# A pool of transposed activations begins 480 bytes further on, and a bias table grows by 32 bytes

## The chip, the cores and the metric

The kernel runs on one core of one Trainium2 chip. The metric is the device time of one execution in microseconds, lower is better. The kernel before takes 1579.77 us (median of three runs, 1577.89 to 1583.2).

## The reference, cut to what matters

One layer of a decoder trunk on 1024 tokens of width 1024, in float32: layer norm, an input projection, two kinds of self-attention side by side, an output projection, cross-attention over 256 memory tokens, and a squared-ReLU MLP of width 4096, each followed by a residual and a layer norm.

```python
x = layer_norm(x, ln_emb_g, ln_emb_b)
h = x @ w_in[l] + b_in[l]
...
mix = jnp.concatenate([out_a, out_b], axis=-1) @ w_o[l] + b_o[l]
x = layer_norm(DN_ALPHA * x + mix, ln1_g[l], ln1_b[l])
ca = memory_cross_attention(x, mem, ...)
x = layer_norm(DN_ALPHA * x + ca, ln2_g[l], ln2_b[l])
f = jnp.square(jax.nn.relu(x @ w_up[l] + b_up[l])) @ w_down[l] + b_down[l]
x = layer_norm(DN_ALPHA * x + f, ln3_g[l], ln3_b[l])
```

## The kernel before

**Arithmetic.** Large products are made of three matmuls each (`mm3`, line 102): a float32 operand is split by ScalarE into a rounded high part, and by GpSimd or VectorE into the rest, the low part; high by high, high by low and low by high are summed in PSUM. In `PE.matmul(out, a, b)` the second operand, `a`, is the stationary one that is loaded as weights (PEld in the profile), and `b` the moving one. In a row of the profile the moving operand stands first: `b<-a,wh` is a moving tile `a` on stationary weights `wh`, `b<-wh,a` a moving tile `wh` on a stationary tile `a`; `b` before the arrow is a PSUM bank. Nearly all matmuls have 512 moving columns; the scores of the cross-attention have 256.

**Stages**, in order of time: input projection and indexer (to about 440 us of the span), the two self-attentions with the memory's projections beside them, the output projection `w_o` and layer norm 1 (about 581 to 700 us), cross-attention for two halves of the tokens (to about 900), `w_up` (about 905 to 1235) and `w_down` (to the end). `w_up` takes 16 steps of seven products of 12 matmuls (`up_product`, line 1096); `w_down` takes three chunks of seven products and a plain rest (`PLAIN`).

**Where tiles lie.** Each partition of on-chip memory is one range of bytes. Pools opened on the left stack upwards, pools on the right downwards. What matters here:

- `pw` (line 131, right): the weights' high parts `wh`, four buffers from byte 188,384, the low parts `wl` from 204,768, and raw weights `wr`. All of them lie 480 bytes beyond a multiple of 512.
- `pm` (line 345, right): `fb0` at 172,000 and `fb1` at 180,192, also 480 beyond a multiple of 512.
- `pact` (line 912, left): the activations, transposed, as `a0` to `a11`, 8,192 bytes each, from byte 71,680, which is 140 times 512. `BIG` (line 916) says that `a0` to `a11` come from `pact` and `fb0`, `fb1` from `pm`; all of them have the same shapes and uses.

- `xT` (line 188, left), the transposed input of the input projection, from byte 50,912, 224 beyond a multiple of 512: 256 bytes from the weights' place.

A slice for one matmul begins at a multiple of 512 bytes within its tile, so a tile's place within 512 bytes is that of all its operands. In `w_o` (`proj_tok`, line 929) and the cross-attention's output, activations are stationary and weights move; in the cross-attention's queries (line 1011) and in `w_up` the weights are stationary and activations move. In `w_up` five of the seven products move two `a` tiles (high and low), and the two with `T3` and `T4` move `fb0` or `fb1` as the high part and an `a` tile as the low part. In the chunks of `w_down` the `a` tiles hold raw quarters that VectorE adds and ScalarE, GpSimd and VectorE split into `wh` and `wl`; only its plain rest gives `a` tiles to TensorE.

**Order.** A planner orders every engine's instructions by a simulated timeline; each engine then runs its own in that order. The pools `pr` and `pact` take over the memory of the self-attention's tiles, each tile waiting for the old tiles that lay under it.

Of the kernel before, what the change touches and what calls it, by code (L numbers as in the profile page):

```python
# [10 lines left out]
F32 = mybir.dt.float32  # L11
# [10 lines left out]
P = 128  # L22
# [12 lines left out]
def kernel(ctx: ExitStack, tc: tile.TileContext, x, mem, ln_emb_g, ln_emb_b, w_in, b_in,  # L35
# [4 lines left out]
    PE, ACT, DVE, POOL, SP = nc.tensor, nc.scalar, nc.vector, nc.gpsimd, nc.sync  # L40
# [4 lines left out]
    def pool(name, bufs=1, **kw):  # L45
        return ctx.enter_context(tc.tile_pool(name=name, bufs=bufs, **kw))

    def sub_pool(name, side=None):
        st = ExitStack()
        kw = {} if side is None else {"side": side}  # L50
        return st, st.enter_context(tc.tile_pool(name=name, bufs=1, reuse_waits="tile", **kw))
# [137 lines left out]
    st0, p0 = sub_pool("p0")  # L189
# [86 lines left out]

    TW = 328
    TC = ((0, 640, 128), (128, 1280, 128), (256, 1920, 72))
    btok = p0.tile([P, TW], F32)
    for d0, s0, n in TC:  # L280
        SP.dma_start(btok[:, d0:d0 + n], row_src(b_in, s0, n))
    th = p0.tile([P, KT, TW], F32R)
# [627 lines left out]
    pst, psum = psum_pool("psd")  # L910
    pr = pool("pr", reuse_waits="tile")
    pact = pool("pact", reuse_waits="tile")
    xr = [pr.tile([P, D], F32, name=f"xr{i}") for i in range(NB)]
    ROW = ("row0", "row1", "row2")
    MM, TR = tuple("b%d" % i for i in range(6)), ("b6", "b7")
# [481 lines left out]
def _build(nc, arrays, inputs, **kw):  # L1397
    import numpy as _np
    args = []
    named = [(n, inputs[n]) for n in _INS] + [("bucket_rows", _bucket_rows())]  # L1400
    for name, v in named:
        a = _np.ascontiguousarray(v)
        arrays[f"in_{name}_dram"] = a
        args.append(nc.dram_tensor(f"in_{name}_dram", a.shape, mybir.dt.from_np(a.dtype), kind="ExternalInput").ap())
    for i, (shape, dtype) in enumerate(_OUTS):
        args.append(nc.dram_tensor(f"out_{i}_dram", shape, mybir.dt.from_np(_np.dtype(dtype)), kind="ExternalOutput").ap())
    with tile.TileContext(nc, schedule_with_timeline_sim=True) as tc:
        kernel(tc, *args, **kw)
# [11 lines left out]
```

## Time and profile before

| | |
|---|---|
| median of three runs | 1579.77 us |
| the profiled execution | 1573.87 us, its span 1572.0 us |
| TensorE matmuls busy | 1449.3 us, 92% of the span |
| VectorE, GpSimd, ScalarE busy | 74%, 54%, 51% |
| granted TensorE clock, mean | 0.967 of full speed |

PE is TensorE's matmuls, PEld its weight loads, DVE VectorE, ACT ScalarE, POOL GpSimd. L86 is the line of `mm` through which nearly all matmuls go, so matmuls are told apart by their tiles. A matmul's recorded duration overlaps those of its neighbours, since they are pipelined; the distance from one start to the next is what a matmul costs in a run of matmuls.

### The profile page before, as it was taken

How to read it: one execution, taken by the hardware profiler on the slowest of the kernel's cores; microseconds unless marked ns; L12 is line 12 of the kernel's file. 1: busy time of each engine (PE TensorE's matmuls, PEld its weight loads, DVE VectorE, ACT ScalarE, POOL GpSimd, SP SyncE). 2: the span in 40 equal slices, each digit the busy share in tenths (PEclk: the TensorE clock that was granted, in tenths of full speed). 3: DMA queues.
4: the chain of work that ended last, by engine and by line, in shares of the span. 5: the costliest groups of instructions: out<-in, count | busy, mean ns of one | idle time of the engine just before them, and what ended most of it. 6: DMA issues, size and time to landing. Idle time of an engine off the chain costs nothing. (4 is left out here: it accounts for less than half of the span.)

```text
span 1572.0 us, 22293 instructions
## 1 busy us (share of the span) xinstructions
PE 1449.3 (92%) x7190; PEld 1208.9 (77%) x7190; DVE 1165.3 (74%) x2442; ACT 798.3 (51%) x1665; POOL 847.4 (54%) x753
## 2 busy tenths in 40 slices
PE   5989998785998999899999979999999999999887
PEld 4877776765897987688888758888888887888666
DVE  8639899969687868985263495575544799988857
ACT  6336677664787864235334154545455444444422
POOL 6213856546556555666565585645445345454745
PEclk9999998986999999999999989999999999999999
DMA  6252445873748248633322133423333934420002
GB/s 218 75 161 68 135 134 154 247 237 93 211 137 241 94 154 267 185 103 105 101 82 84 42 102 121 138 103 129 113 106 100 395 110 134 145 70 1 27 32 103
DMA packets 139907, 206.63 MB, mean 131 GB/s; under 512 B 18055, under 2 KB 83086, under 8 KB 139790
## 3 DMA queue, kind: packets, MB, share of 16 engines
q1 hardware_dynamic: 139790, 205.21, 41.4%
q8 instruction: 57, 0.93, 0.3%
q14 instruction: 60, 0.49, 0.1%
HBM read 151.66 MB, written 52.45 MB: 130 GB/s over the span
## 5 line engine op out<-in xcount | busy, mean ns | idle before, releaser
L86 PE MATMUL b<-a,wh 128*128 128x512 f32 x1072 | 300.2, 402 | 8.8 <-DVE a L1075 8.1
L161 POOL TENSOR_TENSOR wl<-wr,wh 128x512 fp32r<-128x512 f32 x158 | 228.5, 1466 | 145.8 <-ACT wh L160 137.4
L86 PE MATMUL b<-wl,wh 128*128 128x512 f32 x1192 | 278.1, 393 | 13.5 <-POOL wl L1089 13.3
L86 PEld LDWEIGHTS b<-wl,wh 128*128 128x128 f32 x1192 | 224.9, 189 | 63.9 <-POOL wl L1089 16.3
L86 PEld LDWEIGHTS b<-a,wh 128*128 128x128 f32 x1072 | 203.5, 191 | 58.2 <-issue 8.9
L1089 POOL TENSOR_TENSOR wl<-a,wl 128x512 fp32r<-128x512 f32 x44 | 92.4, 2099 | 109.0 <-ACT wl L1088 99.2
L160 ACT ACTIVATE wh<-wr 128x512 fp32r<-128x512 f32 x136 | 81.1, 627 | 128.5 <-PE b L86 46.4
L1089 POOL TENSOR_TENSOR wh<-row,wh 128x512 fp32r<-128x512 f32 x72 | 98.1, 1368 | 88.5 <-ACT wh L1088 85.2
L86 PE MATMUL fill<-xT,wh 128*128 128x512 f32 (+1 forms) x416 | 126.8, 384 | 6.8 <-ACT wt L393 6.8
L86 PE MATMUL b<-wh,a 128*128 128x512 f32 (+1 forms) x416 | 122.5, 369 | 7.6 <-DVE a L761 5.6
L86 PE MATMUL b<-a,wl 128*128 128x512 f32 x400 | 123.0, 396 | 0.0
L1088 ACT ACTIVATE wh<-a 128x512 fp32r<-128x512 f32 x80 | 50.5, 631 | 111.5 <-PE b L86 82.0
L86 PEld LDWEIGHTS fill<-xT,wh 128*128 128x128 f32 x416 | 78.5, 195 | 23.0 <-ACT wt L393 8.3
L86 PEld LDWEIGHTS b<-wh,a 128*128 128x128 f32 x416 | 76.4, 191 | 22.8 <-DVE a L761 5.9
L1282 DVE TENSOR_TENSOR xr<-xr,b 128x512 f32<-128x512 f32 x132 | 81.5, 675 | 14.1 <-PE b L86 14.1
L86 PEld LDWEIGHTS b<-a,wl 128*128 128x128 f32 x400 | 75.0, 188 | 17.4
L86 PE MATMUL fill<-xT,wl 128*128 128x512 f32 (+1 forms) x208 | 79.8, 385 | 0.0
L1100 ACT ACTIVATE lt<-lt,colst 128x512 f32<-128x512 f32 x60 | 43.2, 722 | 68.1 <-DVE lt L1207 67.3
L86 PE MATMUL b<-wl,a 128*128 128x512 f32 (+1 forms) x208 | 76.2, 369 | 1.3 <-POOL wl L161 1.3
L1207 DVE TENSOR_TENSOR lt<-b,lt 128x512 f32<-128x512 f32 x80 | 53.3, 686 | 32.1 <-PE b L86 27.5
L769 DVE TENSOR_TENSOR PT<-tr,PT 128x512 fp32r<-128x512 f32 (+3 forms) x128 | 70.6, 576 | 8.7 <-ACT PT L768 8.4
L768 ACT ACTIVATE PT<-tr 128x512 fp32r<-128x512 f32 (+3 forms) x128 | 61.4, 507 | 25.1 <-PE tr L870 11.6
(327 smaller groups left out, 3664.8 us busy)
## 6 DMA issues: line engine op xcount, KB each, us to landing
row<-in_w_up_dram SPq DMA_DIRECT2D x32, 512.0 KB, 4.3
ff_d<-lt SPq DMA_DIRECT2D x28, 512.0 KB, 3.0
a<-in_w_down_dram SPq DMA_DIRECT2D x50, 256.0 KB, 5.2
a<-ff_d SPq DMA_DIRECT2D x46, 256.0 KB, 3.5
wr<-in_xa_wkv_dram SPq DMA_DIRECT2D x32, 256.0 KB, 4.0
wr<-in_w_o_dram SPq DMA_DIRECT2D x32, 256.0 KB, 3.2
wr<-in_xa_wq_dram SPq DMA_DIRECT2D x32, 256.0 KB, 2.7
wr<-vwo_d SPq DMA_DIRECT2D x32, 256.0 KB, 2.8
```

Source lines behind the costliest of these rows:

```text
L86: i = PE.matmul(o, a, b, start=start, stop=stop)
L160: ACT.activation(hs, raw, AF.Copy)
L161: lo[i % len(lo)].tensor_tensor(out=ls, in0=raw, in1=f(hs), op=OP.subtract)
L768: ACT.activation(PT[0], pt, AF.Copy)
L769: DVE.tensor_tensor(out=PT[1], in0=pt, in1=f(PT[0]), op=OP.subtract)
L1088: ACT.activation(hl[:, 0], raw, AF.Copy)
L1089: return lo.tensor_tensor(out=hl[:, 1], in0=raw, in1=f(hl[:, 0]), op=OP.subtract)
L1100: ACT.activation(c, src, AF.Relu, bias=colst[:, C_UP + col:C_UP + col + 1])
L1207: DVE.tensor_tensor(out=o, in0=a, in1=b, op=op)
L1282: DVE.tensor_tensor(out=xs, in0=xs, in1=p, op=op)
```

## The change

The table of token biases `btok` gets eight more float32 columns, which nothing uses, so every tile of the first stage's pool `p0` that comes after it lies 32 bytes further on. The pool `pact` gets a first tile of 120 float32 (480 bytes) that GpSimd fills with zeros and nothing reads, so `a0` to `a11` begin at byte 72,160, 480 beyond a multiple of 512. `pact` then ends at 170,464, still below `fb0`. The new first tile lies over one old tile, the second query tile `qs` that the last attention unit reads; `a0` lay over it before and still does. No other tile lies over another set of old tiles than before.

```diff
-    btok = p0.tile([P, TW], F32)
+    btok = p0.tile([P, TW + 8], F32, name="btok")[:, :TW]
...
     pact = pool("pact", reuse_waits="tile")
+
+    POOL.memset(pact.tile([P, 120], F32, name="shift"), 0.0)
     xr = [pr.tile([P, D], F32, name=f"xr{i}") for i in range(NB)]
```

## Rows read from the trace of the kernel before

**Rows 1.** The page: span, and each engine's busy time.

```profile
span 1572.0 us, 22293 instructions
PE 1449.3 (92%) x7190; PEld 1208.9 (77%) x7190; DVE 1165.3 (74%) x2442; ACT 798.3 (51%) x1665; POOL 847.4 (54%) x753
```

**Rows 2.** Busy us by stretch (x matmuls started), granted clock as PEclk.

```profile
600.00:700.00 100.00, 91.10 (x399) 72.45 (x399) 92.78 (x108) 37.27 (x58) 65.72 (x38) 0.97 0.55 166
700.00:900.00 200.00, 200.00 (x1020) 167.67 (x1018) 96.90 (x157) 76.43 (x172) 115.18 (x109) 1.00 0.27 88
950.00:1200.00 250.00, 250.00 (x1077) 201.62 (x1076) 143.00 (x186) 126.85 (x208) 125.25 (x92) 1.00 0.35 116
1300.00:1450.00 150.00, 149.78 (x660) 123.91 (x661) 136.43 (x195) 64.12 (x112) 66.86 (x43) 1.00 0.26 87
1450.00:1500.00 50.00, 38.66 (x158) 30.85 (x157) 41.03 (x67) 19.09 (x35) 39.92 (x13) 0.91 0.07 21
```

**Rows 3.** Waits of PE: who for whom, us in total, times, longest.

```profile
PE b L86 <- POOL wl L1089: 13.3, 5, 6.6
```

**Rows 4.** Timeline of PE in `w_o`: start us, us, instruction, count.

```profile
592.27 0.39 PE L86 MATMUL b<-wh 128*128 128x512 f32 x1
...
597.72 0.39 PE L86 MATMUL b<-wh,a 128*128 128x512 f32 x1
...
603.31 0.39 PE L86 MATMUL b<-wh,fb 128*128 128x512 f32 x1
```

**Rows 5.** Timeline of PE in the input projection.

```profile
76.36 0.63 PE L86 MATMUL fill<-xT,wh 128*128 128x512 f32 x2
...
81.82 0.40 PE L86 MATMUL fill<-xT,wh 128*128 128x256 f32 x2
```

**Rows 6.** Timeline of PE in `w_up`.

```profile
1099.82 5.76 PE L86 MATMUL b<-a,wh 128*128 128x512 f32 x24
1105.42 0.40 PE L86 MATMUL b<-fb,wl 128*128 128x512 f32 x1
...
1108.20 5.75 PE L86 MATMUL b<-a,wh 128*128 128x512 f32 x24
```

**Rows 7.** Timeline of PE in `w_down`, one run of matmuls.

```profile
1329.83 110.55 PE L86 MATMUL b<-wl,wh 128*128 128x512 f32 x487
```

**Rows 8.** Timeline of PE in the plain rest of `w_down`.

```profile
1524.16 2.92 PE L86 MATMUL b<-a,a 128*128 128x512 f32 x12
1526.92 0.40 PE L86 MATMUL po<-fb,a 128*128 128x512 f32 x1
...
1529.71 2.92 PE L86 MATMUL b<-a,a 128*128 128x512 f32 x12
```

**Rows 9.** Instructions by form, whole span: xcount | busy us, mean ns | idle before.

```profile
L86 PE MATMUL b<-a,wh 128*128 128x512 f32 x1072 | 300.2, 402 | 8.8 <-DVE a L1075 8.1 <-DVE wr L1071 0.4 <-DVE rstd L116 0.3
L86 PE MATMUL b<-a,wl 128*128 128x512 f32 x400 | 123.0, 396 | 0.0
L86 PE MATMUL b<-wh,a 128*128 128x512 f32 x288 | 95.9, 406 | 7.6 <-DVE a L761 5.6 <-ACT a L760 2.0
L86 PE MATMUL b<-wl,a 128*128 128x512 f32 x144 | 58.2, 406 | 1.3 <-POOL wl L161 1.3
L86 PE MATMUL b<-wh,a 128*128 128x256 f32 x128 | 26.5, 286 | 0.0
L86 PE MATMUL lg<-bb,ident_r 128*128 128x256 f32 x96 | 19.9, 290 | 0.0
```

**Rows 10.** Timeline of POOL: after attention, and late in `w_down`; idle before in brackets.

```profile
587.79 3.37 POOL L161 TENSOR_TENSOR wl<-wr,wh 128x512 fp32r<-128x512 f32 x2 [12.01 <-ACT wh L160]
...
1486.42 11.51 POOL L1089 TENSOR_TENSOR wl<-a,wl 128x512 fp32r<-128x512 f32 x1 [1.60 <-ACT wl L1088]
```

**Rows 11.** DMA issues: xcount, KB each, median us to landing.

```profile
a<-in_w_down_dram SPq DMA_DIRECT2D x50, 256.0 KB, 5.2
fb<-in_w_down_dram SPq DMA_DIRECT2D x6, 256.0 KB, 5.2
```

## The prediction

> **What bounds the kernel now.** I read the page first: matmuls fill 1449.3 us of a span of 1572.0 us, VectorE 74%, GpSimd 54% [rows 1]. TensorE is the first suspect, but an average over stages is no proof, so I took busy time by stretch next [rows 2]. From 700 to 900 us and from 950 to 1200 us TensorE is busy without a break, at full granted clock, with VectorE at about half and GpSimd at 50 to 58%: there, and only there, a shorter matmul is a shorter kernel. From 600 to 700 us it is busy for 91.1 of 100 us. From 1300 to 1450 us it is full as well (149.78 of 150) but VectorE is at 136.43 of 150, so two engines are near their limit. From 1450 to 1500 us it has 38.66 of 50 busy: TensorE waits there, mostly for low parts that GpSimd splits, 13.3 us in five waits [rows 3].
>
> The change touches no work of any size. What it can change is what a matmul costs, so the third view is TensorE's timeline, read for the distance between starts in unbroken runs. The stretch in `w_o` is the best one, since within 11 us, at the same step, with the same kind of moving weights, only the stationary tile changes [rows 4]. From 592.27 to 597.72 us 24 matmuls run with both operands in the weights' own pool: 5.45 us, 227.1 ns each. The next 24, to 603.31 us, have a tile `a` as stationary operand: 5.59 us, 232.9 ns each. So `a` tiles cost about 6 ns a matmul, some 2.5%. With a tile `a` moving instead, `w_up` shows the same: 24 matmuls from 1099.82 to 1105.42 us, 233.3 ns each [rows 6], against 487 in 110.55 us, 227.0 ns each, where both operands are weights' tiles in `w_down` [rows 7].
>
> What sets `a` apart? By the kernel's memory map it is place 0 within 512 bytes against the weights' 480, or that the tile lies in the left half of the memory, or something about activations. The input projection tells these apart: its moving `xT` holds activations and lies on the left as `a` does, but at place 224, which is 480 less 256. 24 matmuls take from 76.36 to 81.82 us, 227.5 ns each [rows 5]. So neither the side nor the contents matter; the place does, it seems, and equal places (at least modulo 256) are the fast ones. After the change `a` is at 480.
>
> **The change part by part.** Durations are of the profiled execution (1573.87 us, span 1572.0 us); the median of the runs lies 5.9 us above it, and I carry savings over one for one.
>
> 1. `w_up`. 16 steps of seven products of 12 matmuls are 1344 matmuls. The stretch from 950 to 1200 us holds 1077 in 250 us, 232.1 ns each; that from 1300 to 1450 us holds 660 in 149.78 busy us, 226.9 ns each, with all operands at 480 [rows 2]. 1344 x 5.2 ns = 7.0 us. The single runs would give more: 960 matmuls of products with `a` alone x 6.3 ns, and 384 in products that mix `fb` and `a` (12 from 1105.42 to 1108.20 us, 231.7 ns each [rows 6]) x 4.7 ns, 7.9 us together. I take 7.0. The first 60 or so of these wait for VectorE's `a` at L1075, 8.1 us in two waits [rows 9], and what they save is waited away: less 0.4.
> 2. The queries of the cross-attention. Of the 1472 matmuls with `a` moving and weights stationary (1072 and 400 [rows 9]) 1088 belong to `w_up`; the other 384, in a stretch without idle time [rows 2], save 6.3 ns each: 2.4 us.
> 3. `a` stationary, weights moving: 288 + 144 = 432 matmuls [rows 9] x 5.9 ns = 2.5 us. Some 240 of them lie in `w_o`, where TensorE has waits (5.6 us of them for VectorE's `a` at L761, which the matmuls do not feed [rows 9]); I drop half of their share, 0.7 us.
> 4. The plain rest of `w_down`, 192 matmuls, half of them with both operands in `a` tiles (12 from 1524.16 to 1526.92 us, 230.0 ns each), half mixed (12 to 1529.71 us, 232.5 ns each) [rows 8]: 96 x 3.0 + 96 x 5.5 ns = 0.8 us.
> 5. The scores of the cross-attention have 256 moving columns on a stationary `a`, 192 of them. Their recorded duration is 286 ns, that of 256-column matmuls with both operands at one place 290 ns [rows 9]: no gain to be seen, perhaps a loss of 192 x 4 ns = 0.8 us. I count the loss; the other end is nothing.
> 6. The memset is one GpSimd instruction of 120 columns. It lies over a query tile of the last attention unit, so it can run when that unit's scores are done. GpSimd is then idle for 12.01 us, waiting for ScalarE's first high part of `w_o` [rows 10]: nothing. Were that cover gone, what queues behind it are those same low parts, which TensorE needs; a 512-column one takes 1.7 us (two in 3.37 [rows 10]), and 120 columns no more than that.
> 7. The 32 bytes in `p0` move `th` and `tl`, whose slices step by 1,312 bytes and so come to eight different places within 512 before and after: nothing on balance.
> 8. The loads of `w_down` now land at place 480 too. `a` at 0 and `fb` at 480 land alike today, 5.2 us each [rows 11]: nothing. [...]
>
> Sum: 7.0 - 0.4 + 2.4 + 2.5 - 0.7 + 0.8 - 0.8 = 10.8 us. 1579.77 - 10.8 = 1569.0 us.
>
> What is late next? In `w_up` no one: VectorE has 143 of 250 us, ScalarE 127, GpSimd 125 [rows 2]. `w_down` keeps its pace, since its operands were at 480 before, and only starts earlier.
>
> Ends of the sum: without both discounts, with 7.9 for `w_up` and without the loss on scores it is 13.6 us (1566.2); if only the two unbroken stretches pay, 6.6 + 2.4 + 1.1 (192 stationary `a` outside `w_o`) - 0.8 = 9.3 us (1570.5). With 2 to 3 us either way for an order of instructions that the planner may lay a little differently, the forecast's own range is 1564 to 1573.
>
> **The rivals.**
>
> No effect. Place is not the cause, and the 6 ns go with something that I haven't separated, such as who wrote the tile. Then nothing is left but a hidden memset: 1579.8 us. Against it stand `xT` [rows 5] and `fb`, which holds the same activations as `a` and, mixed in, is cheaper than `a` alone [rows 6]. [...]
>
> Given back at a chunk's boundary (the one that ends slower). Late in `w_down` one GpSimd split takes 11.51 us [rows 10], where the others take 1.7, while VectorE runs sums and splits without a break; TensorE starves. The stretch from 1450 to 1500 us has 158 matmuls where 220 would fit at 226.9 ns: 62 x 0.227 = 14.1 us lost [rows 2]. `w_down` has three such boundaries, and today only the last one pays that much. Which of GpSimd and VectorE gets in first depends on their relative timing and order, and both may shift: the planner has one more instruction, and TensorE arrives earlier. If one more boundary pays, the time is 1569.0 + 14.1 = 1583.1; if both others do, 1597.2. It decides once more than 10.8 us are lost. Against it: from 1300 to 1450 us GpSimd gets through under a VectorE that is 91% busy.
>
> The same stall goes away. The same dice can fall well: without those 14.1 us the time is 1554.9.
>
> **How the numbers follow.** Forecast 0.62; no effect 0.08; given back 0.18, of which 0.10 one boundary and 0.08 more; stall gone, wholly or in part, 0.12. A measurement of this kernel can tell about 0.3%, 4.7 us, from no change: below 1575.0 is faster, above 1584.5 slower. Faster: 0.62 + 0.12 = 0.74. Within: 0.08 + 0.10 = 0.18. Slower: 0.08. The range takes in no effect and part of the one boundary above, and half of the vanished stall below: 1557 to 1581, which leaves out 0.06 below, and 0.08 + 0.05 above, about 0.19.
>
> **What would show it right or wrong.** Right: in runs as those of [rows 4] and [rows 6] starts lie 227 ns apart with `a` tiles too; 1100 matmuls instead of 1077 in a stretch of 250 us of `w_up`; `w_up` ends some 9 us earlier on the span's clock, and `w_down` takes as long as before. The 256-column scores stay at about 286 to 290 ns. GpSimd's memset falls into its idle time behind the attention. Wrong: starts still 233 ns apart (no effect); or 227 ns, but matmuls missing from some 50 us of `w_down`, with a GpSimd split of 5 us or more beside them (given back); or an attention stage of another length, which would mean that the planner's order has changed more than I think.

## The result and the profile after

The changed kernel takes 1567.76 us (median, 1566.59 to 1569.97) where the kernel before, run beside it, takes 1580.74 us (1577.89 to 1584.41). The ratio is 0.9917, with a 95% interval of 0.9901 to 0.9933: 13.0 us less, with 10.6 to 15.6 us inside the interval. The forecast was 1569.0 us, its own range 1564 to 1573. Two executions at a much lower granted clock, one of `s96` (2331.45 us, 0.563 of full speed) and one of the kernel before (1784.18 us, 0.749), are left out of the ranges and ratios below.

The profiled execution after took 1567.31 us. Its span is only 6.8 us shorter than that of before [rows 1]; where the other half is comes below. The head of its page:

```profile
span 1565.2 us, 22294 instructions
PE 1436.3 (92%) x7190; PEld 1210.2 (77%) x7190; DVE 1166.9 (75%) x2442; ACT 797.0 (51%) x1665; POOL 839.5 (54%) x754
```

The same 7190 matmuls fill 13.0 us less, and there is one GpSimd instruction more. Put side by side, the sequence of instructions on every engine is that of before except for this one (buffer numbers left out), so the two traces can be compared matmul by matmul.

Busy time by stretch of after, columns as in [rows 2] (core time, then PE, PEld, DVE, ACT, POOL with instructions started, granted clock, DMA share, GB/s):

```profile
600.00:700.00 100.00, 91.13 (x406) 73.48 (x405) 92.77 (x109) 38.54 (x59) 61.59 (x38) 0.97 0.56 174
700.00:900.00 200.00, 200.00 (x1036) 170.32 (x1035) 98.59 (x159) 76.42 (x173) 118.05 (x110) 1.00 0.27 88
950.00:1200.00 250.00, 250.00 (x1105) 207.04 (x1104) 145.66 (x190) 128.83 (x214) 129.43 (x97) 1.00 0.36 117
1300.00:1450.00 150.00, 148.05 (x646) 122.02 (x644) 133.77 (x196) 63.96 (x112) 67.56 (x39) 0.99 0.21 71
1450.00:1500.00 50.00, 40.13 (x160) 31.79 (x161) 37.62 (x60) 17.49 (x31) 36.56 (x15) 0.90 0.10 33
```

The unbroken stretches hold more matmuls in the same time: 1105 instead of 1077 in `w_up`, 1036 instead of 1020 in the cross-attention. The window from 1300 to 1450 us holds fewer, 646 instead of 660: the long wait at the last chunk boundary of `w_down` begins inside it now, at 1448.04 us, and began behind it before, at 1454.47 us. That stall is still there (160 matmuls against 158 from 1450 to 1500 us).

TensorE's timeline in `w_o`, against [rows 4]:

```profile
594.08 0.39 PE L86 MATMUL b<-wh 128*128 128x512 f32 x1
...
599.52 0.39 PE L86 MATMUL b<-wh,a 128*128 128x512 f32 x1
...
604.96 0.39 PE L86 MATMUL b<-wh,fb 128*128 128x512 f32 x1
```

24 matmuls from row to row, 5.44 us for both: 226.7 ns with a tile `a` as stationary operand and without one. In `w_up`, against [rows 6]:

```profile
1092.98 5.60 PE L86 MATMUL b<-a,wh 128*128 128x512 f32 x24
1098.42 0.39 PE L86 MATMUL b<-fb,wl 128*128 128x512 f32 x1
...
1101.14 5.60 PE L86 MATMUL b<-a,wh 128*128 128x512 f32 x24
```

24 in 5.44 us and 12 in 2.72 us, 226.7 ns in both products. In the plain rest of `w_down`, against [rows 8]:

```profile
1523.35 2.88 PE L86 MATMUL b<-a,a 128*128 128x512 f32 x12
1526.07 0.39 PE L86 MATMUL po<-fb,a 128*128 128x512 f32 x1
...
1528.79 2.88 PE L86 MATMUL b<-a,a 128*128 128x512 f32 x12
```

12 in 2.72 us for both, 226.7 ns where it was 230.0 and 232.5. By form, against [rows 9], every 512-column form with an `a` tile became shorter, the 256-column ones did not (the last row has no `a` tile and is there for comparison):

```profile
L86 PE MATMUL b<-a,wh 128*128 128x512 f32 x1072 | 293.8, 396 | 9.0 <-DVE a L1077 8.2 <-DVE wr L1073 0.4 <-DVE rstd L116 0.4
L86 PE MATMUL b<-wh,a 128*128 128x512 f32 x288 | 94.3, 400 | 7.1 <-DVE a L761 5.3 <-ACT a L760 1.8
L86 PE MATMUL b<-wh,a 128*128 128x256 f32 x128 | 26.6, 287 | 0.0
L86 PE MATMUL lg<-bb,ident_r 128*128 128x256 f32 x96 | 19.8, 289 | 0.0
```

GpSimd's timeline has the memset at the end of the attention, followed by the idle time that hides it, and the long split of the last chunk boundary, against [rows 10]:

```profile
577.65 0.22 POOL L914 MEMSET shift<- 128x120 f32 x1
589.60 3.14 POOL L161 TENSOR_TENSOR wl<-wr,wh 128x512 fp32r<-128x512 f32 x2 [11.73 <-ACT wh L160]
...
1480.26 11.45 POOL L1091 TENSOR_TENSOR wl<-a,wl 128x512 fp32r<-128x512 f32 x1 [1.65 <-ACT wl L1090]
```

**Where the time went, matmul by matmul.** As the order is the same, the time from the start of the k-th matmul of a trace to that of a later one can be set against the same pair in another trace. Worked out from the starts of all matmuls, in us (counted so that the third of a trace is number 0; `a` at means the place of the `a` tiles within 512 bytes; the experiments are told below):

```
matmuls       what                        before   after  btok_only  s512    s32     s96    s224
3200 - 3400   end of w_o                   45.23   44.17   44.89    44.87   45.08   44.83   44.21
3400 - 4400   cross-attention             195.60  192.88  195.59   195.60  194.06  195.34  192.88
4520 - 5850   w_up                        315.33  307.93  315.10   315.32  311.91  315.12  308.15
6100 - 6200   first boundary of w_down     24.38   28.21   28.21    28.18   28.27   28.16   28.25
7000 - 7180   plain rest of w_down         41.56   40.80   41.56    41.56   41.64   41.26   40.80
```

The four stages that the change touches save 1.06 + 2.72 + 7.40 + 0.76 = 11.9 us, inside the interval of the timed difference. Against that stands the fourth line: at the first chunk boundary of `w_down` the profiled execution of before is 3.83 us shorter than after's. It is the odd one. Kernels whose `a` tiles lie at 0 as in before (`btok_only`, `s512`) take 28.2 us there too, and so do all other profiles but that of `late_dve` below, 26.62 us, whose edit lies behind this stretch. The kernel before isn't shorter there in every execution either: `btok_only`, timed against it, is at 1.0005, 0.9994 to 1.0016, which has no room for 3.8 us.

### The profile page after: what moved, and what is told of

The parts are those of the page before. It is cut to its first block, busy times and chain, and to the rows that moved or that the text cites. A ratio compares the mean times of both kernels' runs of the same rounds, so it can differ in the third digit from the quotient of the medians.

```text
span 1565.2 us, 22294 instructions
## 1 busy us (share of the span) xinstructions
PE 1436.3 (92%) x7190; PEld 1210.2 (77%) x7190; DVE 1166.9 (75%) x2442; ACT 797.0 (51%) x1665; POOL 839.5 (54%) x754
## 5 line engine op out<-in xcount | busy, mean ns | idle before, releaser
L86 PE MATMUL b<-a,wh 128*128 128x512 f32 x1072 | 293.8, 396 | 9.0 <-DVE a L1077 8.2
L161 POOL TENSOR_TENSOR wl<-wr,wh 128x512 fp32r<-128x512 f32 x158 | 225.2, 1443 | 142.8 <-ACT wh L160 129.2
L768 ACT ACTIVATE PT<-tr 128x512 fp32r<-128x512 f32 (+3 forms) x128 | 61.6, 507 | 26.1 <-PE tr L870 10.9
```

Of the source, the lines that this page charges most:

```text
L86: i = PE.matmul(o, a, b, start=start, stop=stop)
L161: lo[i % len(lo)].tensor_tensor(out=ls, in0=raw, in1=f(hs), op=OP.subtract)
L768: ACT.activation(PT[0], pt, AF.Copy)
```

## The experiments

All are edits of the changed kernel; the lines of a diff with "+" are the experiment's. A ratio is against the kernel before, run on the same chip beside it.

### Is it the place, or the memset and the move itself?

The first tile of `pact` gets 512 bytes instead of 480, so `a` lies at 0 again: the same instructions, the same order, every tile moved.

```diff
-    POOL.memset(pact.tile([P, 120], F32, name="shift"), 0.0)
+    POOL.memset(pact.tile([P, 128], F32, name="shift"), 0.0)
```

> The pad at the head of the pool has 128 columns (512 bytes) instead of 120, so the a tiles are back at place 0 within 512 bytes; the memset, the longer bias table and every engine's order are those of the changed kernel. Place theory: no gain, 1580 us as before, starts in w_up 233 ns apart, about 1077 matmuls in 250 us of w_up. Order theory (the memset or the bias table shifts the relative timing of the engines): the gain stays, 1568 us.

Measured: 1578.92 us (1573.92 to 1585.7), ratio 1.0004, 0.9989 to 1.0019. Its stretch of `w_up`:

```profile
950.00:1200.00 250.00, 250.00 (x1077) 201.60 (x1076) 142.85 (x186) 127.62 (x208) 124.01 (x93) 1.00 0.35 116
```

1077 matmuls, the number of before to the last one [rows 2], and `w_up` as long as before in the table. The whole gain hangs on where the `a` tiles lie within 512 bytes. The rival "no effect" falls, and with it any account by the memset or by a move as such.

### One part alone

Only the bias table, with the memset taken out:

```diff
-    POOL.memset(pact.tile([P, 120], F32, name="shift"), 0.0)
```

> The longer bias table alone. Place theory: no effect, 1580 us, within 0.2% of before; attention as long as before. If the 32 bytes in the first stage matter, up to some us either way.

Measured: 1580.0 us (1574.14 to 1583.97), ratio 1.0005, 0.9994 to 1.0016.

Only the pool, with the bias table as before:

```diff
-    btok = p0.tile([P, TW + 8], F32, name="btok")[:, :TW]
+    btok = p0.tile([P, TW], F32)
```

> The 480 bytes at the head of the pool alone, without the longer bias table. Place theory: the whole gain, 1568 us (ratio 0.992). If the bias table has a share, less than that.

Measured: 1572.24 us (1569.09 to 1573.22), ratio 0.9954, 0.994 to 0.9968. That is 3.7 parts in a thousand short of the whole change, as if the table had a share when the pool is moved too. The traces showed no such share (`w_up` and the cross-attention as long as in after), so both were run again, side by side on one chip.

> The 480 bytes at the head of the pool alone, a second time. It was 1572.2 us beside 1567.8 us of the whole change. If the longer bias table has a share of the gain that shows only together with the moved pool: 1572 us again, some 4 us over the whole change beside it. If that was chance: equal to the whole change within 2 us.

> The whole change, a second time, on the chip of the run with the pool alone: 1568 us by every theory; its distance to that run is what counts.

Measured: the pool alone 1566.25 us (1562.83 to 1570.53), ratio 0.9915, 0.9896 to 0.9933; the whole change 1569.64 us (1564.25 to 1571.66), ratio 0.9937, 0.9919 to 0.9956. Now the part alone is the shorter one. The two sets of one kernel lie 6 us apart, on two chips, more than their intervals say; whether chance or the chip made that is open. In the profile of the first set 3.4 us of it can be placed: the matmuls 6700 to 7000, at the last boundary of `w_down`, take 88.00 us, against 84.61 in after and 84.85 in the second set. The table's 32 bytes have no share that these runs can show.

### Equal places, or equal modulo 256, or only nearer?

`a` at 224, 256 bytes from the weights' place, as `xT` lies:

```diff
-    POOL.memset(pact.tile([P, 120], F32, name="shift"), 0.0)
+    POOL.memset(pact.tile([P, 56], F32, name="shift"), 0.0)
```

> The pad has 56 columns: the a tiles lie at place 224 within 512 bytes, 256 away from the weights' 480. If equal places modulo 256 are enough (as xT at 224 in the input projection suggests): 1568 us, starts 227 ns apart in w_up. If the places must be equal within 512: 1580 us, 233 ns.

Measured: 1567.5 us (1565.18 to 1571.81), ratio 0.9931, 0.9915 to 0.9947: the whole gain. Its stretch of `w_up`:

```profile
950.00:1200.00 250.00, 250.00 (x1104) 206.69 (x1103) 144.60 (x189) 129.80 (x214) 128.53 (x96) 1.00 0.36 117
```

It was run again without the table's 32 bytes.

```diff
-    btok = p0.tile([P, TW + 8], F32, name="btok")[:, :TW]
+    btok = p0.tile([P, TW], F32)
...
-    POOL.memset(pact.tile([P, 120], F32, name="shift"), 0.0)
+    POOL.memset(pact.tile([P, 56], F32, name="shift"), 0.0)
```

> A pad of 56 columns (a tiles at place 224) without the longer bias table; with it the time was 1567.5 us. If the table has a share: about 1572 us. If not: 1567.5 us.

Measured: 1568.4 us (1565.29 to 1571.76), ratio 0.9932, 0.9914 to 0.995. The same.

`a` at 96, 384 bytes from the weights' place and 128 modulo 256 (a first tile of 24 columns):

```diff
-    POOL.memset(pact.tile([P, 120], F32, name="shift"), 0.0)
+    POOL.memset(pact.tile([P, 24], F32, name="shift"), 0.0)
```

> The pad has 24 columns: the a tiles lie at place 96, equal to the weights' 480 modulo 128 but not modulo 256. If equality modulo 128 is enough: 1568 us, starts 227 ns apart in w_up. If it takes 256: 1580 us, 233 ns or what this distance costs.

Measured: 1577.07 us (1574.86 to 1584.36), ratio 0.9986, 0.9971 to 1.0001: next to nothing. `a` at 32, which is 64 bytes beyond the weights' place modulo 512 (8 columns):

```diff
-    POOL.memset(pact.tile([P, 120], F32, name="shift"), 0.0)
+    POOL.memset(pact.tile([P, 8], F32, name="shift"), 0.0)
```

> The pad has 8 columns: the a tiles lie at place 32, equal to the weights' 480 modulo 64 but not modulo 128. If place 0 itself is what costs (a theory of one operand alone) or equality modulo 64 is enough: 1568 us and 227 ns. If the two operands' places must be equal modulo 128 or more: 1580 us and about 233 ns.

Measured: 1574.05 us (1573.1 to 1574.32), ratio 0.9959, 0.9944 to 0.9975: half the gain. Its timeline in `w_up`:

```profile
1104.38 5.67 PE L86 MATMUL b<-a,wh 128*128 128x512 f32 x24
1109.89 0.40 PE L86 MATMUL b<-fb,wl 128*128 128x512 f32 x1
```

24 in 5.51 us, 229.6 ns, between the 233.3 of [rows 6] and the 226.7 of after. The mean distance from the start of a 512-column matmul to the next start, by the place of its moving operand and that of the next matmul's stationary one, worked out from all starts of each trace that lie at most 260 ns apart, with the number of pairs:

```
place of a    a moving, weights at 480     weights moving, a stationary    both a (plain rest)
0  (before)       233.2 ns  x1403               233.0 ns  x461                230.6 ns  x141
0  (s512)         233.2     x1410               232.9     x465                230.6     x141
32                229.7     x1401               233.1     x457                231.2     x141
96                232.1     x1401               232.2     x464                229.3     x141
224               227.1     x1406               227.4     x465                226.8     x141
480 (after)       227.1     x1404               227.3     x461                227.0     x141
```

Counted modulo 256, a moving `a` at 0, 32 or 96 lies 32, 64 or 128 bytes ahead of the weights' 480. In the first two columns equal places modulo 256 are the fast ones, and the other distances tried cost some 5 to 6 ns, but for a moving operand 64 bytes ahead, which costs 2.6. As stationary operand the same tiles cost the full 6. The last column shows that equality is not all: there both operands lie at one place in every row, and yet 0, 32 and 96 cost 2 to 4 ns more than 224 and 480.

### Is there something special about 480?

Activations, `fb` and weights all at 384, by a pool of 96 bytes on the right ahead of `pw` and a first tile of 384 bytes in `pact`. Only `xT` stays at 224, now 160 bytes from the weights, or 96 ahead of them modulo 256.

```diff
+    pad = pool("pad", side="right")
+    POOL.memset(pad.tile([P, 24], F32, name="pad"), 0.0)
     pw = pool("pw", side="right")
...
-    POOL.memset(pact.tile([P, 120], F32, name="shift"), 0.0)
+    POOL.memset(pact.tile([P, 96], F32, name="shift"), 0.0)
```

> Weights, fb and a tiles all lie at place 384 (a pad of 96 bytes under the weights' pools, 96 columns at the head of the a tiles' pool); xT stays at 224, which is now another place than the weights'. Theory of equal places: w_up and w_down keep 227 ns, and the input projection's runs of xT on weights go from 227 to about 233 ns: 528 matmuls x 6 ns = 3 us at most, 1568 to 1571 us. Theory that 480 (or 224) is a good place for an operand by itself: all of w_up and w_down at 233 ns or more, some 20 us slower, 1588 us.

Measured: 1569.85 us (1567.92 to 1571.72), ratio 0.9932, 0.9916 to 0.9947. All pairs at 384 are 227.1 ns apart (3736 pairs), as at 480. And the matmuls that were fast before the change are slow now. The input projection, against [rows 5]:

```profile
77.08 0.63 PE L86 MATMUL fill<-xT,wh 128*128 128x512 f32 x2
...
82.68 0.40 PE L86 MATMUL fill<-xT,wh 128*128 128x256 f32 x2
```

24 in 5.60 us, 233.3 ns, where it was 227.5. `xT` itself has not moved, and its contents are the same; the weights have moved. So for these matmuls it is the relation of the two operands, not the place of either.

### The stall that stayed

GpSimd's split of 11.45 us, above, stands beside a VectorE that is busy almost all through. The same stretch by engine, columns as before:

```profile
1480.26:1491.71 11.45, 8.02 (x36) 6.31 (x34) 10.33 (x18) 2.31 (x4) 11.45 (x2) 1.00 0.00 1
```

But a busy VectorE alone doesn't hold GpSimd up. Just before this stretch, VectorE sums eight results of TensorE without a gap, with one operand from PSUM, the memory that matmuls write, and one from SBUF, the on-chip memory that holds the tiles told of above, and GpSimd passes beside them:

```profile
1474.88 4.87 DVE L1284 TENSOR_TENSOR xr<-xr,b 128x512 f32<-128x512 f32 x8
```

```profile
1467.57 8.54 POOL L1091 TENSOR_TENSOR wl<-a,wl 128x512 fp32r<-128x512 f32 x1 [3.42 <-ACT wl L1090]
1476.07 1.29 POOL L1091 TENSOR_TENSOR wh<-a,wh 128x512 fp32r<-128x512 f32 x1
1477.31 1.30 POOL L1091 TENSOR_TENSOR wl<-a,wl 128x512 fp32r<-128x512 f32 x1
```

The three longest GpSimd instructions of this stretch (7.61 us from 1443.26, 8.54 and 11.45 us) stand beside VectorE's sums and splits that read both operands from SBUF, and each ends 1.1 us after the last of an unbroken run of those. Such a run doesn't always win: at the first boundary the two engines take turns, and VectorE's instructions are stretched from 0.7 to 1.8 us instead.

```profile
1295.69 1.78 DVE L1091 TENSOR_TENSOR wh<-fb,wh 128x512 fp32r<-128x512 f32 x1
```

```profile
1295.18 1.74 POOL L1091 TENSOR_TENSOR wh<-a,wh 128x512 fp32r<-128x512 f32 x1
```

What decides between the two isn't shown.

What TensorE waits for from 1400 to 1520 us in after (us in total, times, longest):

```profile
PE b L86 <- POOL wl L1091: 12.0, 5, 6.5
```

The longest of the five waits, 6.53 us, ends at 1454.58 us; it lies behind the 7.61 us instruction and three more that GpSimd had to do after it. The wait behind the split of 11.45 us is 3.48 us.

If GpSimd only waits there behind VectorE, its work is done sooner on VectorE, where a split takes 0.7 us in after. From the fifth step of the last chunk on, all low parts go to VectorE:

```diff
+    late = []
+
     def lo_engine():
+        if late:
+            return DVE
         nlo[0] += 1
...
         for s, (sums, a, b, outs, done) in enumerate(steps):
+            if c == len(CHUNKS) - 1 and s == 4:
+                late.append(True)
```

> The changed kernel, but from the fifth product of the last chunk of w_down on all low parts are computed by VectorE instead of three in eight by GpSimd. If TensorE's idle time about 1450 to 1500 us comes from GpSimd's splits waiting behind VectorE's sums (one of 11.5 us): those waits go, at the price of some 20 splits more on VectorE at 0.6 us, most of them beside matmuls: 1556 to 1564 us. If VectorE's own work is the limit there: 1568 us or a little more.

Measured: 1562.7 us (1556.85 to 1565.74), ratio 0.9886, 0.9867 to 0.9906: clearly shorter than the kernel before, and shorter than after by the medians. The intervals of the two ratios overlap (after has 0.9901 to 0.9933), and its slowest execution lies below the fastest of after's first set (1566.59), though not of its second (1564.25), so that the gain over after rests on the traces more than on the times. Its last stretch and its waits of TensorE from 1400 to 1520 us:

```profile
1450.00:1500.00 50.00, 46.77 (x197) 37.56 (x196) 50.00 (x84) 21.75 (x38) 0.00 (x0) 0.97 0.08 27
```

```profile
PE b L86 <- DVE wl L1091: 3.2, 3, 2.0
```

197 matmuls instead of 160, and VectorE, with twenty splits more, is full for the whole 50 us; GpSimd stands still. Taken matmul by matmul, 6700 to 7000 take 73.75 us instead of 84.60, and the time from the 7180th to the end of VectorE's last instruction is 9.58 us instead of 7.28, so the vectors' work after the last matmuls became longer. (The planner laid some matmuls in another order here, all of them between 6950 and 7060.) A version that hands over one step later:

```diff
-            if c == len(CHUNKS) - 1 and s == 4:
+            if c == len(CHUNKS) - 1 and s == 5:
```

> As the run with late low parts on VectorE, but from the sixth product of the last chunk instead of the fifth, so some five splits fewer move to VectorE. If GpSimd's waits in the last two products are all that was gained: 1562 us again or 1 to 2 us less; if a GpSimd split of the fifth product already waits long: some us more.

Measured, in four executions: 1563.98 us (1560.29 to 1565.14), ratio 0.9901, 0.9881 to 0.9921. No better; the two can't be told apart.

## Why the prediction was right

The forecast of 1569.0 us stands 1.2 us from the time measured. So near a hit is partly luck: the six sets of executions with `a` at 480 or 224 have ratios of 0.9915 to 0.9954, 7 to 13 us, with a mean of 10.9 us. The relation, equal places modulo 256, held for 512-column matmuls in each run that could have broken it (233 ns in `s512`, 227 in `s224`, 227 at equal and 233 at unequal places in `both384`) wherever one operand is an `a` tile or `xT` and the other a weights' tile. It doesn't cover matmuls with both operands in `a` tiles (step 4). By its own steps:

1. **`w_up`.** 7.0 less 0.4 was predicted; 7.40 us came, on the matmuls 4520 to 5850. The mis-sized term is the price of one matmul. I took 5.2 ns from two windows, of which one lies in another stage and counts whole matmuls; from 4600 to 5800 it is 6.99 us / 1200 = 5.8 ns, and the single runs of [rows 6] had said 7.9 / 1344 = 5.9. The other profiles with `a` at 480 or 224 take 0 to 0.7 us more than after for these matmuls, nearly all of it in two neighbouring starts, and agree with it elsewhere. The discount of 0.4 for the first matmuls was right in kind: the 80 from 4520 on saved at most 0.28 us (24.87 to 24.59) of 80 x 5.8 ns = 0.46, and `btok_only` alone, where nothing can be saved, took 24.64.
2. **The queries, and 3, `a` as stationary operand, with 5, the scores.** Predicted 2.4 + 1.8 - 0.8 = 3.4 us; from matmul 3200 to 4400 it is 1.06 + 2.72 = 3.78 us. The 116 stationary ones from 3000 to 3200 are not in that; this stage took from 54.5 to 57.5 us in the profiles, and so hides their 0.7 us. The loss of 0.8 us on the scores did not come: 287 ns against 286, and starts 118.7 ns apart against 118.4 (156 pairs each).
4. **The plain rest.** Predicted 0.8, measured 0.76. But the prediction's rule doesn't give the half with both operands in `a` tiles: their places are equal before (0 and 0) and after (480 and 480), so it should have saved nothing. I took its 3.0 ns from [rows 8] without noticing that those rows speak against equality as the whole rule. The 3 ns came (230.0 to 226.7), and why is open.
6. **The memset.** 0.22 us, ahead of 11.73 us of idle time. Nothing, as predicted.
7. **The 32 bytes in the first pool.** Nothing, as predicted: 1.0005, 0.9994 to 1.0016.
8. **The loads of `w_down`.** They take 5.4 us to land, for `a` and for `fb` alike, against 5.2 before [rows 11]. Nobody waits for them longer: the run of 648 matmuls at 1299 us goes through without a break.

The sum of the stages is 11.9 us instead of 10.8; most of the difference is the price in `w_up` and the loss that I counted on the scores.

**The rivals.** "No effect" would have needed starts still 233 ns apart. Here 24 matmuls of `w_up` take 5.60 us at unequal places (before [rows 6]) and 5.44 us at equal ones (after), and `s512`, which has the instructions and the order of after and `a` at 0, is at 233.2 ns against after's 227.1. So the measurement decides against it.

"Given back" seemed to have come true at first sight, and this was the reading that needed most care. TensorE's timeline of after at the first chunk boundary:

```profile
1223.55 64.97 PE L86 MATMUL b<-wl,wh 128*128 128x512 f32 x285
1289.38 7.76 PE L86 MATMUL b<-wl,wh 128*128 128x512 f32 x31 [0.86 <-POOL wl L1091]
1299.19 148.85 PE L86 MATMUL b<-wl,wh 128*128 128x512 f32 x648 [2.05 <-DVE wl L1091]
```

and of `btok_only`, with `a` at 0 as before:

```profile
1229.34 65.03 PE L86 MATMUL b<-wl,wh 128*128 128x512 f32 x285
1295.21 7.79 PE L86 MATMUL b<-wl,wh 128*128 128x512 f32 x31 [0.83 <-POOL wl L1089]
1305.04 148.85 PE L86 MATMUL b<-wl,wh 128*128 128x512 f32 x648 [2.04 <-DVE wl L1089]
```

The waits are the same to some hundredths of a us, 5.8 us earlier on the clock. So this boundary is paid without the change too, and the profiled execution of before happened to get by more cheaply. That was also the execution with the shortest time of those that the prediction had, 1573.87 us against a median of 1579.77, and 6.9 us under the median that was then measured beside after. Of these 6.9, 3.83 lie at this boundary and about 1.8 in the attention stage (the first matmul of `w_o` starts at 583.12 us in after, 581.30 before, with nothing changed ahead of it but the bias table, which by itself changes no time, and the hidden memset). With the same order of instructions that start lies anywhere from 577.47 us (`btok_only`) to 587.37 (the second run of after), so an attention stage of another length, which the prediction named as a sign of being wrong, is no sign of anything here. I had carried savings from that execution to the median one for one. That was right, since the stages that save have hardly any idle time in either; comparing the two spans alone would have said 6.8 us, half of what the medians say.

The prediction's reading of the last boundary was off in two points. The split of 11.51 us was not the only long one in before: another took 8.30 us from 1474.01 us. And the argument against "given back", that GpSimd gets through under a VectorE that is 91% busy, doesn't carry over to the last boundary: in before 71 of VectorE's 195 instructions from 1300 to 1450 us are sums from PSUM, and none of the 18 beside the split of 11.45 us in after is. That which of the two gets in first can change with the order kept, as the prediction assumed, the traces do show: the GpSimd split that takes 1.76 us at 1293.46 us in after, with VectorE's next instruction stretched to 1.77, takes 2.52 us at 1304.29 us in before, with VectorE's beside it at 0.67. That the relative timing decides it is my estimate.

"The same stall goes away" did not happen by itself (160 matmuls against 158), but `late_dve` made part of it happen. It gained 5.1 us on the medians of its kernel and of after, not 14.1. TensorE got 10.85 us back at the boundary (84.60 to 73.75), but VectorE then had 50.00 of 50 us to do, and the end came 2.3 us later behind the last matmuls. In the profiled executions another 3.0 us went before anything that the edit touches: matmul 6700 starts at 1431.79 us in `late_dve` and at 1428.77 in after.

## What to carry to other kernels

Compare the starts of consecutive matmuls between stages that do the same work: 2.5% per matmul is invisible in busy shares, and plain in a run of 24. Where a kernel is bound by 512-column float32r matmuls, try moving and stationary operands at the same place modulo 256 bytes, and more than one such place; here 480 bytes of padding ahead of a pool were all it took. And before a difference between two profiled executions is put down to a change, look whether a kernel that keeps the old cause shows it too.

## What the runs showed of the hardware

- The distance between starts of 512-column matmuls depends on the operands' places relative to each other: 227 ns at equal places modulo 256, 232 to 233 ns at most others tried, 229.7 ns with the moving operand 64 bytes ahead. For 256-column matmuls on a stationary `a` the same move gains nothing (118.4 ns with `a` at 0, 118.7 at 480), but place is not without effect there: 115.6 ns at 32 and 119.7 at 96.
- Both operands in `a` tiles at 0, 32 or 96 give 229 to 231 ns, at 224, 384 or 480 they give 227. This is seen only in the plain rest of `w_down`, in 141 pairs for each place, and its reason stays open. So does the reason for the whole effect: the runs show the relation, not what in the chip makes it.
- One GpSimd split of 512 columns, which takes 1.3 us beside VectorE instructions that read one operand from PSUM, took 11.45 us beside some 18 that read both from SBUF, with hardly a gap between them. The trace of after shows two ways in which the two engines meet: turn by turn at the first boundary (1.7 to 1.8 us for each instruction of either engine), and here GpSimd passed over not once but through the whole run of VectorE, until 1.1 us after its end. Why the two hold each other up, and what decides between the two ways, isn't shown.
- Medians of six executions of one kernel differed by more than their intervals: 1572.24 and 1566.25 us for the pool alone, on two chips, 0.9954 and 0.9915 against before. A third of a per cent in one set of this kernel is no finding without a second one.
